# Gated projections of half a sequence as seven products of quarters instead of four plain ones per tile

## The chip, the cores and the metric

The kernel runs on one core of a Trainium2 chip. The metric is the device time of one execution in microseconds; the time before is the median of three runs. One further execution was profiled, and every row shown below comes from it. The engines are named as the profile names them: PE is TensorE, PEld its weight loads, DVE VectorE, ACT ScalarE, POOL GpSimd, SP the engine whose queue issues nearly all transfers.

## The reference

One decoder block on 2048 tokens of 1024 features, float32. What matters here is how two branches are joined:

```python
proj = h @ w_in[l]
q, k, v, z_a, u_b, v_b, z_b, g_logits = jnp.split(proj, SPLIT_IDX, axis=-1)
...
y_a = _swa_with_sinks(q, k, v, sinks[l]) * jax.nn.silu(z_a)      # 2048 x 512
y_b = ...  # spatial gating of u_b, v_b, times silu(z_b)          # 2048 x 512
gate_a, gate_b = jnp.split(jax.nn.sigmoid(g_logits), 2, axis=-1)
merged = gate_a * (y_a @ w_proj_a[l]) + gate_b * (y_b @ w_proj_b[l])
y = merged @ w_out[l]
x = x + gate * _rms(y, g_post[l])
```

## The kernel before

*Numbers.* Each float32 operand of a large product is split into a high part, rounded to the format that TensorE multiplies in, and a low part, the rest. A weight is split into a tile `W` (`w_of`: ScalarE casts the high part, L215; VectorE subtracts it for the low part, `sub`, L150), an activation into a tile `T` (`t_load`: casts at L373, subtractions at L150). A product of two 128x128 by 128x512 blocks is three matmuls: high by high, high by low, low by high (`mm3`, L167). The low part of `W` is first needed by the third.

*Stages.* The sequence is worked in two halves of 1024 tokens. (1) Two passes over `w_in`, one for each half, in 19 blocks of 256 output features. Each block is a product of 2x2 quarters by a scheme of seven products instead of eight (Strassen's, in Winograd's form): sums of quarters of the weight stand in `sS`, sums of quarters of the activation in `hT`; four PSUM banks X, Y, Z, W collect the products in the order of `BANK`, and ScalarE copies partial sums between banks (L418). The attention and the spatial gating of a half run beside its pass, hung on it with `later`. The last two blocks of a pass (`NLAST`) alternate product by product, with two banks each (`two_banks`), and the T tiles of what follows are loaded beside them. (2) The gated projections, first for the first half of the tokens, then for the second: the loop `for s in range(NS)` in `run_all`. (3) The output product with `w_out`, again by seven products, tile by tile of 128 rows of `merged` (`m_s`), with the norm and the final sum in `ev_out`.

*The projections.* For each of the eight feature tiles `j` there are four products of 12 matmuls: `y_a` and `y_b`, each for two groups of 512 tokens. One weight `W` serves two of them. When a product is done, `gated` (L1143) multiplies it on VectorE with one plus its gate tile; `g_load` has fetched the gate tiles into tags `m` and `e`. `merge` adds the gated `a` and `b` on VectorE and stores the sum to `m_s`. Four T tiles serve all eight `j`; the next four are loaded during the loop.

*Order.* Every engine works its own queue in the order in which the code emits instructions. One product is a *step*; `later(n, f)` emits `f` n steps on. At the start of step k the code takes the weight for it and prepares that of step k+3: ScalarE's cast is emitted then, VectorE's subtraction (`due`) one step later. There are four `W` buffers, eight for raw weights, ten for loads of T (`x`). Sums of weight quarters for a fresh (not stored) block are made by GpSimd in stage 3 (`psub`, L153).

Of the kernel before, what the change touches and what calls it, by code (L numbers as in the profile page):

```python
# [15 lines left out]
P = 128  # L16
D = 1024
# [38 lines left out]
def hybrid_block(ctx: ExitStack, tc: tile.TileContext, xt, x, wada, wgate, wI, wP, wO,  # L56
# [46 lines left out]
    sS = [[dram(f"sS{n}_{i}", [P, 512]) for i in range(4)] for n in range(NPAIR)]  # L103
    hT = [[dram(f"hT{p}_{kt}", [P, 512]) for kt in range(4)] for p in range(7)]
    oT = {p: [dram(f"oT{p}_{kt}", [P, 512]) for kt in range(4)] for p in (1, 2, 4, 6)}
# [207 lines left out]
    def presum(n):  # L313

        env, q = {}, wI_quads(n)
# [31 lines left out]
    for s in range(NS):  # L347
# [35 lines left out]
    class Block:  # L383
# [33 lines left out]
        def copy(self, to, of):  # L417
            act.copy(self.b[to], self.b[of])  # L418

# [706 lines left out]

    def o_src(p):
# [22 lines left out]
    def run_all():  # L1150
        nonlocal T

        for s in range(NS):
# [17 lines left out]
            if s == 0:  # L1171
# [5 lines left out]
                for i in range(NLAST):  # L1177
                    later(91 + 10 * i, lambda i=i: presum(NPAIR - NLAST + i))
            else:
                for kk in range(KT):  # L1180
# [3 lines left out]
                for kt in range(4):  # L1184
                    later(86 + 8 * kt, lambda kt=kt: o_step(kt))
# [65 lines left out]
        for s in range(NS):  # L1251
            Y4, nT = T, [None] * 7
            g_load(s, 0)
            for j in range(KT):
# [5 lines left out]
                for p in range(4):  # L1260
# [4 lines left out]
                    if s == 0:  # L1265
                        if j in (1, 2, 3) and p == 0:
                            t_load(nT, j - 1, 2, yab(1, j - 1))
                        elif j == KT - 1 and p == 0:
                            t_load(nT, 3, 1, yab(1, 3))
                    elif j in (2, 3, 4) and p == 0:  # L1270
# [24 lines left out]
    def ev_out(s, i):  # L1295
# [11 lines left out]
        def ev(key, src, psum):  # L1307
# [6 lines left out]
            if len(ys) == 2:  # L1314
                later(1, lambda: scale_of(r))

        def scale_of(r):
            xr, ss, ys = st[r]
            e0, v, ry = small(1, "e0"), small(1, "pw"), small(1, "ry")

            pool.tensor_scalar(out=e0, in0=ss[:, 0:1], scalar1=1.0 / D, scalar2=16.0 * EPS, op0=ALU.mult, op1=ALU.add)
            pool.tensor_scalar(out=v, in0=ss[:, 1:2], scalar1=1.0 / D, scalar2=e0, op0=ALU.mult, op1=ALU.add)
            pool.tensor_tensor(out=ry, in0=v, in1=nhalf[:, 0:1], op=ALU.pow)
            later(1, lambda: finish(r, ry))

        def finish(r, ry):
            xr, ss, ys = st[r]
            row = s * 8 + r * 4 + i
            for f in range(2):
# [90 lines left out]
```

## Time and profile before

| | |
|---|---|
| median of 3 runs | 1220.93 us (1220.47 to 1221.25) |
| the profiled execution | 1220.76 us, its span 1219.1 us, granted clock 0.997 |
| input pass, second half, to the first projection | until 885.1 us |
| projections, first half | 885.1 to 972.2 us |
| projections, second half | 972.2 to 1059.2 us |
| output product | 1059.2 to 1211.7 us |
| busy: TensorE, VectorE, ScalarE, GpSimd | 1199.3, 834.4, 607.5, 274.7 us |

A row of the timeline is the start, the duration, the engine, the line and operation, what it writes and reads, and how many equal ones it merges; in brackets stands the idle time before it and what ended it. Durations include a tail of some 0.08 us that overlaps with the next operation, so the spacing of starts tells what a queue costs. A matmul's duration is that of its way through the array: twelve that start 2.72 us before the next twelve are shown with 2.88.

### The profile page before, as it was taken

The numbers are of one execution on the slowest core, as the hardware profiler recorded it, in microseconds if no ns is written. First come the engines' busy times: TensorE is split into PE (matmuls) and PEld (weight loads), VectorE is DVE, ScalarE is ACT, GpSimd is POOL, SyncE is SP. The second block draws the span as 40 slices with busy tenths as digits, with TensorE's granted clock in tenths as the row PEclk, the third lists the DMA queues.
The fourth block names the chain that finished last, engine by engine and source line by source line (L and its number), as shares of the span: only waits on it lengthen the run. The fifth ranks groups of instructions, "written<-read, shape, count | busy, mean of one in ns | idle before, by whom it ended". The sixth has DMA issues, their size and how long they took to land.

```text
span 1219.1 us, 17154 instructions
## 1 busy us (share of the span) xinstructions
PE 1199.3 (98%) x5496; PEld 955.8 (78%) x5496; DVE 834.4 (68%) x1289; ACT 607.5 (50%) x1321; POOL 274.7 (23%) x246
## 2 busy tenths in 40 slices
PE   8999999999999999999999999999999999999997
PEld 3667887877777777888888787777788888888886
DVE  7996979667867666358757676555656556767775
ACT  4475454576765676434346665555622112444443
POOL 0002654323465200013200002210000000155443
PEclk9999999999999999999999999999999999999999
DMA  9545998867999996569795679888797677845452
GB/s 352 225 148 188 318 320 288 247 153 199 312 337 333 326 317 234 169 225 301 232 291 169 173 206 299 264 262 255 246 299 236 224 251 232 285 156 178 133 181 87
DMA packets 215506, 294.15 MB, mean 241 GB/s; under 512 B 19828, under 2 KB 96244, under 8 KB 215416
## 3 DMA queue, kind: packets, MB, share of 16 engines
q1 hardware_dynamic: 214944, 292.37, 74.7%
q8 instruction: 43, 0.70, 0.2%
q0 software_dynamic: 176, 0.53, 0.1%
q14 instruction: 47, 0.39, 0.1%
q10 hardware_dynamic: 296, 0.16, 0.1%
HBM read 189.50 MB, written 98.24 MB: 236 GB/s over the span
## 4 chain that ended last, share of the span: by engine, by line
PE 88%; DVE 5%; DMA 3%; ACT 2%; issue 1%; DVEq 0%; ACTq 0%; SPq 0%
PE bankY L167 28%; PE bankX L167 20%; PE bankW L167 12%; PE bankZ L167 12%; PE s L167 4%; PE b L167 4%; PE b L1009 2%; PE s L959 2%; DMA T<-in_wada 1%; PE s L960 1%; PE b L898 1%; PE b L994 1%; DVE W L150 1%; DMA raw<-in_wI 1%; DVE T L661 1%
## 5 line engine op out<-in xcount | busy, mean ns | idle before, releaser
L167 PE MATMUL bankY<-T,W 128*128 128x512 f32 x1608 | 390.5, 392 | 0.9 <-ACT bankZ L418 0.6
L167 PEld LDWEIGHTS bankY<-T,W 128*128 128x128 f32 x1608 | 299.3, 188 | 64.4 <-ACT bankZ L418 1.0
L150 DVE TENSOR_TENSOR W<-raw,W 128x512 fp32r<-128x512 f32 x320 | 255.1, 801 | 71.3 <-ACT W L215 71.1
L215 ACT CAST W<-raw 128x512 fp32r<-128x512 f32 x320 | 197.6, 618 | 169.5 <-PE b L167 53.2
L167 PE MATMUL bankX<-T,W 128*128 128x512 f32 x1140 | 279.7, 393 | 1.8 <-DVE T L661 1.7
L167 PEld LDWEIGHTS bankX<-T,W 128*128 128x128 f32 x1140 | 211.1, 188 | 48.1 <-DVE T L661 5.0
L167 PE MATMUL bankW<-T,W 128*128 128x512 f32 x708 | 175.8, 394 | 4.1 <-DVE T L661 2.5
L167 PE MATMUL bankZ<-T,W 128*128 128x512 f32 x708 | 171.0, 390 | 0.0
L167 PEld LDWEIGHTS bankW<-T,W 128*128 128x128 f32 x708 | 130.4, 188 | 36.5 <-DVE T L661 4.7
L167 PEld LDWEIGHTS bankZ<-T,W 128*128 128x128 f32 x708 | 132.2, 188 | 27.3
L153 POOL TENSOR_TENSOR S<-raw,raw 128x512 f32<-128x512 f32 x22 | 34.4, 1564 | 254.5 <-DMA raw<-m 200.0
L153 POOL TENSOR_TENSOR raw<-raw,raw 128x512 f32<-128x512 f32 x44 | 69.3, 1575 | 87.0 <-DVE W L150 36.6
L153 POOL TENSOR_TENSOR S<-x,x 128x512 f32<-128x512 f32 x18 | 24.5, 1366 | 218.9 <-DMA x<-in_wO 199.1
L156 DVE TENSOR_TENSOR e<-bankY,e 128x512 f32<-128x512 f32 x41 | 28.2, 689 | 63.7 <-PE bankY L167 63.6
L150 DVE TENSOR_TENSOR T<-x,T 128x512 fp32r<-128x512 f32 (+1 forms) x93 | 60.8, 695 | 9.7 <-ACT T L373 9.7
L167 PE MATMUL s<-T,W 128*128 128x512 f32 x276 | 66.4, 389 | 0.0
L167 PEld LDWEIGHTS s<-T,W 128*128 128x128 f32 x276 | 51.7, 188 | 10.7
L153 POOL TENSOR_TENSOR raw<-S,raw 128x512 f32<-128x512 f32 x22 | 32.3, 1469 | 116.8 <-DVE W L150 87.6
L373 ACT CAST T<-x 128x512 fp32r<-128x512 f32 x88 | 48.8, 618 | 4.2 <-PE s L167 4.2
L988 ACT ACTIVATE P<-P,rc 128x128 f32<-128x128 f32 x128 | 44.5, 396 | 11.4 <-DVE rc L984 11.1
L146 POOL TENSOR_SCALAR pw<-mv 128x1 f32<-128x1 f32 x16 | 6.6, 414 | 185.4 <-DVE mv L782 185.3
L979 ACT ACTIVATE P<-s,nb 128x129 f32<-128x129 f32 x128 | 46.0, 366 | 1.0 <-DVE nb L971 0.8
(236 smaller groups left out, 1380.9 us busy)
## 6 DMA issues: line engine op xcount, KB each, us to landing
raw<-in_wI SPq DMA_DIRECT2D x128, 256.0 KB, 4.3
raw<-sS SPq DMA_DIRECT2D x84, 256.0 KB, 4.4
g<-e SPq DMA_DIRECT2D x64, 256.0 KB, 3.9
sS<-raw SPq DMA_DIRECT2D x45, 256.0 KB, 4.4
T<-in_wada SPq DMA_DIRECT2D x16, 512.0 KB, 8.4
q<-q SPq DMA_DIRECT2D x64, 128.0 KB, 5.5
q<-k_s SPq DMA_DIRECT2D x64, 128.0 KB, 4.9
raw<-in_wP SPq DMA_DIRECT2D x32, 256.0 KB, 3.8
```

The source lines that it names most:

```text
L150: dve.tensor_tensor(out=o, in0=a, in1=b, op=ALU.subtract)
L153: pool.tensor_tensor(out=o, in0=a, in1=b, op=op)
L156: dve.tensor_tensor(out=o, in0=a, in1=b, op=ALU.add)
L167: pe.matmul(o, w[:, i, sl], t[:, j, kt, :], start=start and kt == kts[0] and n == 0, stop=stop and kt == last and n == 2, skip_group_check ...
L215: act.copy(w[:, 0, :], src)
L373: act.copy(T[p][:, 0, kt, :], rs[kt])
L661: dve.scalar_tensor_tensor(out=T[p][:, 1, kt, :], in0=t_src(p, kt), scalar=sh, in1=T[p][:, 0, kt, :].bitcast(F32), op0=ALU.add, op1=ALU.su ...
L898: pe.matmul(b[:, ch * P : (ch + 1) * P], st["v", h][:, ch, :], wT[:, c, :], start=True, stop=True)
L959: pe.matmul(o, q[:, g, :], k[:, 0, :], start=True, stop=False)
L979: act.activation(out=st["P", kv][:, g, :], in_=st["S", kv][:, g, 0 : P + 1], func=AF.Exp, scale=SM, bias=st["nb", kv][:, g : g + 1], accum ...
L988: act.activation(out=st["P", kv][:, g, 0:P], in_=st["P", kv][:, g, 0:P], func=AF.Copy, scale=st["rc", kv][:, g : g + 1])
L1009: pe.matmul(o[own, :], v[:, k, own], st["pv", kv][k], start=k == 1, stop=k == 0)
```

## The change

The projections of the first half (s = 0) are now made like the blocks of the passes. Features go in pairs of tiles (`Pair`, n = 0 to 3), tokens in two groups of 512, the inner dimension in two quarters of 256, so 2x2 quarters and seven products, each of six matmuls for `y_a` and six for `y_b`, side by side in banks of their own. Pairs 0 and 1 follow one another with four banks for each side, their weight sums made by GpSimd on the way; pairs 2 and 3 alternate with two banks for each side, their weight sums made earlier by `presum` (at steps 1 and 82 of the second pass) and stored. The sums of quarters of `y_a` and `y_b` (`pT`) are made by GpSimd in steps 9 to 20 of the second pass (`y_step`) and stored. The last two blocks of that pass now load seven T tiles instead of four. The sum of the two gated tiles moves from VectorE to GpSimd (`psub` in `out`), and gate tiles go into tags `m`, `S` and `q`. `o_step` is spread a little differently. In `ev_out` the two parts of the norm's sum are scaled by GpSimd as they come, and at the very end of the kernel the first row block is finished before the last multiplication. The projections of the second half stay as they were.

```diff
+    def p_quads(n):
+        return {f"A{f + 1}{k + 1}": wP[2 * n + f][:, :, 256 * k : 256 * (k + 1)].rearrange("a p c -> p a c")
+                for f in range(2) for k in range(2)}
...
-    for s in range(NS):
+    for n in range(2):
+        stream_fresh(p_quads(n))
+    for n in range(2, 4):
+        stream_stored(p_quads(n), NPAIR + n - 2)
+    by_product(2)
+    for s in range(1, NS):
...
+    class Pair:
...
+        def run(self, p, w, T):
+            early = self.two
+            if p >= 1 + early and p < 5 + early:
+                self.gates(("11", "22", "12", "21")[p - 1 - early])
+            if self.n == 0 and p == 0:
+                for z in "YZ":
+                    pe.matmul(self.b[1][z], w[:, 0, 0:P], T[p][:, 0, 0, :], start=True, stop=True, skip_group_check=True)
+            for ab in range(2):
+                mm3(self.b[ab][BANK[p]], w, T[p], (2 * ab, 2 * ab + 1), FRESH[p], True)
+                if ab == 0:
+                    do_hooks("mid")
...
+            elif p == 1:
+                self.wsb = [flat("e") for _ in both]
+                if self.two:
+                    dve.tensor_copy(self.wsb[0], self.b[0]["W"])
+                    act.copy(self.wsb[1], self.b[1]["W"])
+                    self.copy("Y", "X")
...
+            elif p == 3:
+                self.out("11", [self.b[ab]["X"] for ab in both])
+                if self.two:
+                    self.copy("Z", "Y")
+            elif p == 4:
+                c = [flat("e") for _ in both]
+                for ab in both:
+                    add(c[ab], self.b[ab]["Y"], self.wsb[ab])
+                self.out("22", c)
+            elif p == 5:
+                for ab in both:
+                    add(self.wsb[ab], self.b[ab]["Z"], self.wsb[ab])
+                self.out("12", self.wsb)
+            else:
+                self.out("21", [self.b[ab]["Y"] for ab in both])
...
+        def out(self, key, src):
+            ga, gb = (self.g.pop((key, ab)) for ab in range(2))
+            gated(ga, src[0])
+            gated(gb, src[1])
+            psub(ga, ga, gb, ALU.add)
+            store(1, m_s[half(key)][:, 2 * self.n + ft(key), :], ga)
...
+    def y_step(i):
+        hs = []
+        for k in (i % 2, i % 2 + 2):
+            for h in range(2):
+                hs.append(flat("x"))
+                sp.dma_start(hs[-1], (ya_s, yb_s)[i // 2][h][:, k, :])
+        keep_T(pT, i, hs, False, 3)
...
+                for i in range(4):
+                    later(6 + 3 * i, lambda i=i: y_step(i))
+                for i in range(2):
+                    later((1, 82)[i], lambda i=i: presum(NPAIR + i, p_quads(2 + i)))
...
-                elif p < 4:
-                    t_load(nT, p, 2, yab(0, p))
+                else:
+                    t_load(nT, p, 2, p_src(p))
...
+        for n in range(2):
+            c = banks()
+            blk = Pair(n, (BK, {"X": c[0], "Y": c[1], "Z": c[2], "W": c[3]}))
+            for p in range(7):
+                w = w_get()
+                step(lambda: blk.run(p, w, T))
+        c = banks()
+        blks = [Pair(2, (two_banks(BK["X"], BK["W"]), two_banks(BK["Y"], BK["Z"]))),
+                Pair(3, (two_banks(c[0], c[1]), two_banks(c[2], c[3])))]
+        nT = [None] * 7
+        for p in range(7):
+            if p < 4:
+                t_load(nT, p, 2, yab(1, p))
+            if p == 6:
+                g_load(1, 0)
+            for i in range(2):
+                w = w_get()
+                step(lambda: blks[i].run(p, w, T))
...
+            if r == 0 and s == NS - 1 and i == 3:
+                later(0, lambda: finish(r, ry), "mid")
+            else:
+                later(1, lambda: finish(r, ry))
```

What this does to the queues shows best where the pairs alternate. First TensorE. Before, in the projections of the first half; `s` and `b` are PSUM tiles beside the four fixed banks:

```order
L167 MATMUL bankX<-T_8355,W_8923 128x512 x12
L167 MATMUL bankY<-T_8439,W_8923 128x512 x12
L167 MATMUL bankZ<-T_8506,W_8975 128x512 x12
L167 MATMUL bankW<-T_8566,W_8975 128x512 x12
L167 MATMUL s_9139<-T_8355,W_9017 128x512 x12
```

Now, products 6 to 9 of the 14 of pairs 2 and 3 (counted from 0):

```order
L168 MATMUL bankX<-T_8712,W_9316 128x512 x6
L168 MATMUL bankY<-T_8712,W_9316 128x512 x6
L168 MATMUL s_9233<-T_8712,W_9351 128x512 x6
L168 MATMUL b_9234<-T_8712,W_9351 128x512 x6
L168 MATMUL bankW<-T_8778,W_9377 128x512 x6
L168 MATMUL bankZ<-T_8778,W_9377 128x512 x6
L168 MATMUL s_9233<-T_8778,W_9410 128x512 x6
L168 MATMUL b_9235<-T_8778,W_9410 128x512 x6
```

Twelve matmuls still share a weight, but the weight serves one step of twelve where it served two, and the T tile changes with every second step.

Then VectorE. Before, over the four products of a tile `j` beside which a T tile is split (`T<-x,T`):

```order
L1143 SCALAR_TENSOR_TENSOR m_8855<-m_8855,bankX 128x512
L150 TENSOR_TENSOR W_8881<-raw_8690,W_8881 128x512
L1143 SCALAR_TENSOR_TENSOR m_8859<-m_8859,bankY 128x512
L150 TENSOR_TENSOR T_8927<-x_8885,T_8927 128x512
L150 TENSOR_TENSOR T_8927<-x_8887,T_8927 128x512
L1143 SCALAR_TENSOR_TENSOR e_8856<-e_8856,bankZ 128x512
L150 TENSOR_TENSOR T_8927<-x_8889,T_8927 128x512
L150 TENSOR_TENSOR T_8927<-x_8891,T_8927 128x512
L150 TENSOR_TENSOR W_8923<-raw_8719,W_8923 128x512
L156 TENSOR_TENSOR m_8855<-m_8855,e_8856 128x512
L1143 SCALAR_TENSOR_TENSOR e_8860<-e_8860,bankW 128x512
L156 TENSOR_TENSOR m_8859<-m_8859,e_8860 128x512
```

Now, in products 8 and 9 of pairs 2 and 3, up to the split of the weight for product 12 (`W_9506`):

```order
L1236 SCALAR_TENSOR_TENSOR S_9417<-S_9417,e_9496 128x512
L1236 SCALAR_TENSOR_TENSOR q_9419<-q_9419,e_9497 128x512
L151 TENSOR_TENSOR W_9472<-raw_9318,W_9472 128x512
L151 TENSOR_TENSOR T_9476<-x_9401,T_9476 128x512
L151 TENSOR_TENSOR T_9476<-x_9403,T_9476 128x512
L157 TENSOR_TENSOR e_9529<-s_9233,e_9334 128x512
L157 TENSOR_TENSOR e_9530<-b_9235,e_9335 128x512
L1236 SCALAR_TENSOR_TENSOR S_9448<-S_9448,e_9529 128x512
L1236 SCALAR_TENSOR_TENSOR q_9450<-q_9450,e_9530 128x512
L151 TENSOR_TENSOR T_9476<-x_9405,T_9476 128x512
L151 TENSOR_TENSOR T_9476<-x_9407,T_9476 128x512
L151 TENSOR_TENSOR W_9506<-raw_9353,W_9506 128x512
```

The twelve rows of before belong to four products, the twelve of now to less than two. The sum of the gated tiles is gone from this queue and stands in GpSimd's, which had nothing between the sums for `w_out` and those for stage 3; these are the last two of pair 1 and the first four of pairs 2 and 3:

```order
L154 TENSOR_TENSOR m_9141<-m_9141,q_9143 128x512
L154 TENSOR_TENSOR S_9166<-S_9166,q_9168 128x512
L154 TENSOR_TENSOR m_9358<-m_9358,q_9360 128x512
L154 TENSOR_TENSOR m_9383<-m_9383,q_9385 128x512
L154 TENSOR_TENSOR S_9417<-S_9417,q_9419 128x512
L154 TENSOR_TENSOR S_9448<-S_9448,q_9450 128x512
```

Each of them follows a pair of gatings on VectorE, and the store of the sum follows it in SP's queue.

More of the change, by code (lines that the diff above doesn't have):

```diff
@@ L418, in copy, with __init__, gates @@
             act.copy(self.b[to], self.b[of])
+    class Pair:
+        def __init__(self, n, banks):
+            self.n, self.b, self.two = n, banks, banks[0]["W"] is banks[0]["Y"]
+            self.g = {}
+        def gates(self, key):
+            j, h = 2 * self.n + ft(key), half(key)
+            tags = ("m" if key[0] == "1" else "S", "q")
+            for ab in range(2):
+                t = self.g[key, ab] = flat(tags[ab])
+                sp.dma_start(t, g_s[8 * ab + j][h])
+        def run(self, p, w, T):
[5 more added lines that the diff above has]
+                    pe.matmul(self.b[1][z], w[:, 0, 0:P], T[p][:, 0, 0, :], start=True, stop=True, skip_group_check=True)
+            for ab in range(2):
+                mm3(self.b[ab][BANK[p]], w, T[p], (2 * ab, 2 * ab + 1), FRESH[p], True)
+                if ab == 0:
+                    do_hooks("mid")
+            both = range(2)
+            if p == 0:
+                if not self.two:
+                    self.copy("Y", "X")
[4 more added lines that the diff above has]
+                    act.copy(self.wsb[1], self.b[1]["W"])
+                    self.copy("Y", "X")
+                else:
+                    for ab in both:
+                        act.copy(self.wsb[ab], self.b[ab]["W"])
+            elif p == 2:
+                if not self.two:
+                    self.copy("Z", "Y")
+            elif p == 3:
+                self.out("11", [self.b[ab]["X"] for ab in both])
+                if self.two:
+                    self.copy("Z", "Y")
+            elif p == 4:
[4 more added lines that the diff above has]
+            elif p == 5:
+                for ab in both:
+                    add(self.wsb[ab], self.b[ab]["Z"], self.wsb[ab])
+                self.out("12", self.wsb)
+            else:
+                self.out("21", [self.b[ab]["Y"] for ab in both])
+        def copy(self, to, of):
+            for ab in range(2):
+                act.copy(self.b[ab][to], self.b[ab][of])
+        def out(self, key, src):
[4 more added lines that the diff above has]
+            store(1, m_s[half(key)][:, 2 * self.n + ft(key), :], ga)
@@ L1125, in yab, with p_src @@
         return [src[:, kt, :] for kt in range(4)]
+    def p_src(p):
+        if p in (1, 2, 4, 6):
+            return pT[p]
+        k, h = {0: (0, 0), 3: (1, 0), 5: (1, 1)}[p]
+        return [z[h][:, 2 * k + i, :] for z in (ya_s, yb_s) for i in range(2)]
+    def y_step(i):
[5 more added lines that the diff above has]
+        keep_T(pT, i, hs, False, 3)
     def o_src(p):
@@ L1184, in run_all @@
                 for kt in range(4):
-                    later(86 + 8 * kt, lambda kt=kt: o_step(kt))
+                    later(90 + 7 * kt, lambda kt=kt: o_step(kt))
             n0 = 0
@@ L1249, in run_all, with banks @@
             T = nT
-        for s in range(NS):
+        def banks():
+            S = pS.tile([P, 2, 512], F32, tag="s", name=nm("s"))
+            return S[:, 0, :], S[:, 1, :], bank(), bank()
+        for n in range(2):
[16 more added lines that the diff above has]
+                step(lambda: blks[i].run(p, w, T))
+        T = nT
+        for s in range(1, NS):
             Y4, nT = T, [None] * 7
-            g_load(s, 0)
             for j in range(KT):
@@ L1328, in finish @@
             row = s * 8 + r * 4 + i
-            for f in range(2):
+            for f in (r, 1 - r):
                 dve.scalar_tensor_tensor(out=xr[f], in0=ys[f], scalar=ry, in1=xr[f], op0=ALU.mult, op1=ALU.add)
```

33 lines of the change are left out of this document (16 added, 17 removed).

## The prediction

> **What bounds the kernel now.** I read the busy table and the chain first, then busy time by stage, then TensorE's rows in the stage that changes, and then VectorE's rows, because they show what could take TensorE's place.
>
> ```profile
> PE 1199.3 (98%) x5496; PEld 955.8 (78%) x5496; DVE 834.4 (68%) x1289; ACT 607.5 (50%) x1321; POOL 274.7 (23%) x246
> ...
> PE 88%; DVE 5%; DMA 3%; ACT 2%; issue 1%; DVEq 0%; ACTq 0%; SPq 0%
> ```
>
> TensorE is busy in 98% of the span and carries 88% of the chain. A matmul that goes away is time gained, unless TensorE then waits.
>
> ```profile
> 885.10:972.20 87.10, 87.10 (x386) 72.09 (x385) 50.25 (x78) 18.89 (x33) 0.00 (x0) 1.00 0.78 253
> ...
> 431.00:469.30 38.30, 38.30 (x175) 29.19 (x174) 30.87 (x54) 30.23 (x68) 0.00 (x0) 1.00 0.95 321
> ```
>
> The columns after the length are the busy time of TensorE, its weight loads, VectorE, ScalarE and GpSimd, then clock, share of the DMA engines and GB/s. 885 to 972 us is the projection stage of the first half: TensorE without a pause, VectorE at 58%, GpSimd idle. 431 to 469 us is the last pair of input blocks of the first half, fourteen products with seven T tiles loaded beside them: 321 GB/s at a share of 0.95, and still TensorE has no gap.
>
> ```profile
> 885.13 2.88 PE L167 MATMUL bankX<-T,W 128*128 128x512 f32 x12
> ...
> 969.46 2.88 PE L167 MATMUL b<-T,W 128*128 128x512 f32 x12
> 972.17 2.88 PE L167 MATMUL bankX<-T,W 128*128 128x512 f32 x12
> ```
>
> The first product of the stage starts at 885.13 and the first of the next stage at 972.17: 87.04 us for 32 groups of 12 matmuls, 2.72 us a group, 0.2267 us a matmul.
>
> **The change, part by part.**
>
> 1. *Matmuls.* Before, 8 feature tiles x 4 products x 12 = 384. After, 4 pairs x 7 products x 12 = 336, and 2 that only set up the banks Y and Z of the second side: 46 fewer. 46 x 0.2267 = 10.43 us less on TensorE, all of it on the chain.
>
> 2. *Sums of T, loads of T, sums of weights.* Sixteen GpSimd subtractions and eight weight sums move into the second input pass, and its last pair now loads seven T instead of four. The row of 431 us is that same load in the first half, T loads included, and it hid it. What is new there are four GpSimd sums for the first pair; each can take up to 1.10 us from VectorE (below), 4.4 us together, in 38.3 us of which VectorE was idle 7.4 (38.30 less 30.87). I take 0 and keep 1 us for the range.
>
> 3. *VectorE in the last two pairs.* This is the only stretch where I find it short. Pairs 2 and 3 alternate, 14 products. Call the start of the first one 0; product k ends at 2.72(k+1). VectorE has 14 splits of W, 16 of T, 16 gatings, 8 additions from PSUM and 2 copies: 56 operations. In a closed queue one follows another every 0.60 us, whatever it reads:
>
> ```profile
> 441.54 2.49 DVE L150 TENSOR_TENSOR T<-x,T 128x512 fp32r<-128x512 f32 x4
> 443.95 0.68 DVE L150 TENSOR_TENSOR W<-raw,W 128x512 fp32r<-128x512 f32 x1
> ...
> 460.98 1.28 DVE L150 TENSOR_TENSOR T<-x,T 128x512 fp32r<-128x512 f32 x2
> 462.18 0.68 DVE L156 TENSOR_TENSOR e<-bankY,e 128x512 f32<-128x512 f32 x1
> 462.78 1.28 DVE L150 TENSOR_TENSOR T<-x,T 128x512 fp32r<-128x512 f32 x2
> ```
>
> ```profile
> 1056.99 0.68 DVE L1143 SCALAR_TENSOR_TENSOR e<-e,s 128x512 f32<-128x512 f32 x1
> 1057.59 1.28 DVE L150 TENSOR_TENSOR T<-x,T 128x512 fp32r<-128x512 f32 x2
> ```
>
> Four splits of T take 443.95 - 441.54 = 2.41 us, the PSUM addition at 462.18 is followed at 462.78, the gating at 1056.99 at 1057.59. 56 x 0.60 = 33.6 of 38.1 us; but the splits of T lie in products 3 to 9 and all gatings come from product 6 on. The code hands VectorE the split of product m's W after the outputs of product m-3, and TensorE needs it at its third matmul, so the queue may run 5.4 + 0.45 us behind. From the end of product 6 (19.04, and 0.2 us until PSUM is read) to the split for product 12 stand 24 operations: 19.24 + 24 x 0.60 = 33.64, wanted at 12 x 2.72 + 0.45 = 33.09. TensorE waits 0.55. Each of the next two splits comes 5 operations (3.0 us) later where a product takes 2.72: 0.28 more each, 1.1 us in all. That is the low end.
>
> 4. *GpSimd's additions among them.* After each pair of gatings GpSimd now adds the two tiles (before, VectorE did, 0.60 us each). What that costs VectorE is in these rows:
>
> ```profile
> 593.71 5.95 POOL L153 TENSOR_TENSOR x<-x,m 128x512 f32<-128x512 f32 x4
> ...
> 595.03 1.77 DVE L156 TENSOR_TENSOR x<-x,x 128x512 f32<-128x512 f32 x1 [0.46 <-POOL x L153]
> 596.72 1.78 DVE L150 TENSOR_TENSOR W<-raw,W 128x512 fp32r<-128x512 f32 x1
> 598.42 1.77 DVE L806 TENSOR_TENSOR e<-e,m 128x512 f32<-128x512 f32 x1
> 600.12 0.67 DVE L870 SCALAR_TENSOR_TENSOR e<-e,bankX 128x512 f32<-128x512 f32 x1
> 600.72 0.68 DVE L150 TENSOR_TENSOR W<-raw,W 128x512 fp32r<-128x512 f32 x1
> ```
>
> While GpSimd worked through four operations on SBUF, VectorE's operations with both inputs in SBUF started 1.70 us apart instead of 0.60, one for each of GpSimd's: 1.10 us lost each time. One that reads PSUM loses nothing:
>
> ```profile
> 300.12 0.68 DVE L999 TENSOR_TENSOR m<-b,cst 128x512 f32<-128x512 f32 x1
> 300.17 1.29 POOL L153 TENSOR_TENSOR S<-x,x 128x512 f32<-128x512 f32 x1 [4.26 <-ACT x L1058]
> 300.83 0.69 DVE L150 TENSOR_TENSOR m<-b,m 128x512 f32<-128x512 f32 x1
> ```
>
> The two VectorE rows take 0.68 and 0.69 us under a GpSimd operation that runs from 300.17 to 301.46. Once in the trace it was GpSimd that waited:
>
> ```profile
> 1063.61 1.28 DVE L150 TENSOR_TENSOR T<-x,T 128x512 fp32r<-128x512 f32 x2
> 1063.82 4.63 POOL L153 TENSOR_TENSOR raw<-raw,raw 128x512 f32<-128x512 f32 x1 [14.96 <-DVE W L150]
> ...
> 1065.41 1.28 DVE L150 TENSOR_TENSOR T<-x,T 128x512 fp32r<-128x512 f32 x2
> 1066.62 0.68 DVE L150 TENSOR_TENSOR W<-raw,W 128x512 fp32r<-128x512 f32 x1
> 1068.41 1.29 POOL L153 TENSOR_TENSOR S<-raw,raw 128x512 f32<-128x512 f32 x1
> ```
>
> Here VectorE's queue was closed, its operations stayed at 0.68 or 1.28 for two, and GpSimd's took 4.63 us, until the queue had a gap. So the price of an addition lies between 0 and 1.10 us. Four of the eight come before the split for product 12 and meet splits of T and W with both inputs in SBUF; the four after it meet additions from PSUM. I take 1.10, because the slowed rows recur and the other stands alone: 4 x 1.10 = 4.4 us, and the wait grows from 1.1 to 5.5 us. [...]
>
> 5. *PSUM copies.* Each pair needs 2 copies from X to Y, 2 of W out and 2 from Y to Z on ScalarE.
>
> ```profile
> 1054.56 4.32 ACT L373 CAST T<-x 128x512 fp32r<-128x512 f32 x8
> ...
> 1062.13 0.57 ACT L418 COPY bankY<-bankX 128x512 f32<-128x512 f32 x1 [1.06 <-PE bankX L167]
> ```
>
> A copy takes 0.57 us and eight casts of T 4.32, so 0.54 each. In the interleaved pairs the W and Y copies after a product (3 x 0.57) have the partner's product, 2.72 us, to hide in, with at most two casts of T between them: 1.71 + 0.54 + 0.2 = 2.45. The Z copies wait for the gatings of product 6; with VectorE not yet late there they are ready at about 21.1, the next product wants them at 21.76. For product 9 they come 0.1 to 0.2 us late, which the 5.5 us already hold, since VectorE's queue runs on meanwhile. Pairs 0 and 1 do not alternate, but have four banks for each side; the second side of pair 1 starts when the last gating of pair 0 has read its bank, about when TensorE arrives (20.4 us from the start of pair 0 by both counts). I take 0 and keep 0.8 for the range.
>
> 6. *The end.*
>
> ```profile
> 1208.81 2.88 PE L167 MATMUL bankY<-T,W 128*128 128x512 f32 x12
> ...
> 1211.40 0.55 POOL L1323 TENSOR_TENSOR ry<-pw,nhalf 128x1 f32<-128x1 f32 x1
> ...
> 1212.51 0.69 DVE L1313 TENSOR_TENSOR e<-bankY,rg 128x512 f32<-128x512 f32 x1 [1.33 <-ACT m L1311]
> 1212.57 0.19 POOL L1321 TENSOR_SCALAR e<-yss 128x1 f32<-128x1 f32 x1 [0.62 <-ACT m L1311]
> 1212.86 0.26 POOL L1322 TENSOR_SCALAR pw<-yss,e 128x1 f32<-128x1 f32 x1
> 1213.12 2.73 DVE L1330 SCALAR_TENSOR_TENSOR x<-e,ry,x 128x512 f32<-128x512 f32 x4
> 1213.21 1.06 POOL L1323 TENSOR_TENSOR ry<-pw,nhalf 128x1 f32<-128x1 f32 x1
> ```
>
> The last matmul ends at 1211.69. VectorE then does one multiplication (1212.51) and four final operations (1213.12 to 1215.85), though the factor of the first two was ready at 1211.95. Now these two stand ahead of the multiplication, and GpSimd's tail is an operation shorter (0.29 us from 1212.57 to 1212.86): the last factor is there at 1213.98 instead of 1214.27, and 2 x 0.68 later, at 1215.35, all is done. That gains 0.5 us; the bounds are 0 and 0.8.
>
> Sum, on the profiled execution's 1220.76 us (span 1219.1): -10.43 + 5.5 - 0.5 = -5.4. The median of the runs is 0.17 above that execution: 1220.93 - 5.4 = 1215.5 us.
>
> **The rivals.**
>
> *GpSimd yields.* Its additions fall into VectorE's gaps, as at 1063.82; the wait is 1.1 us. 1220.93 - 10.43 + 1.1 - 0.5 = 1211.1. Against it stand the three rows from 595 on.
>
> *The DMA queue fills.* In products 4 to 11 of the alternating pairs some 37 transfers of 262 KB start (16 gates, 8 T, 8 weights, 5 stores), 9.7 MB. At the rate of the 431 us row (321 GB/s at 0.95, so 338 full) that takes 28.7 us where 21.8 pass: up to 6.9 us late.
>
> ```profile
> m<-g SPq DMA_DIRECT2D x32, 256.0 KB, 3.6
> ...
> m<-m SPq DMA_DIRECT2D x32, 256.0 KB, 2.8
> ...
> x<-ya SPq DMA_DIRECT2D x16, 256.0 KB, 5.2
> ```
>
> T loads start 5.4 us ahead and took 5.2, so they have no reserve; but ScalarE reaches their casts later than that (the second T some 8 us after its load), and nothing needs these T before the next stage. Half of the lateness, 3.4 us, on top of the sum: 1218.9.
>
> *Slower than before: gates behind stores.* SyncE's queue is in order. A store of a sum waits for GpSimd, which waits for VectorE, and the next gate loads stand behind it; VectorE in turn stops at a gating whose gate has not landed, with the splits of W behind that. A loop of landing (3.6), store and wait could put VectorE further back at every product. TensorE must lose 10.9 us before the change is slower than nothing, so 5.4 beyond part 4; with the full 6.9 us late at the gates it ends at 1222.4. For it: each gate tile of a pair has a store ahead of it. Against it: the first gates are asked for in product 4 and used after product 6, 8.2 us ahead of a landing of 3.6, and the later ones are wanted by a VectorE that is itself late.
>
> **How the numbers follow.** My forecast, additions at full price: 0.48. GpSimd yields: 0.27. The DMA queue: 0.14. The loop: 0.07. What I do not see: 0.04. A difference under 0.2% (2.4 us) can't be told from none. The forecast and the yielding case lie beyond that, with half of the DMA case: 0.82 faster; most of the rest of the DMA case and part of the unseen, 0.10, the same; the loop and the rest, 0.08, slower. The range runs from 1210.5, just under the yielding case with the end at its best, to 1219.0, over the DMA case; it leaves out the loop, the upper part of the DMA case and a little below, 0.18 together.
>
> **What would show it.** Right: the products of the four pairs 2.72 us apart but for gaps in TensorE from product 12 of the alternating pairs on, released by the split of W on VectorE, 4 to 6 us in all; splits there 1.7 us apart beside GpSimd's additions; no gap in the second input pass; the final four operations done about 3.7 us after the last matmul instead of 4.2. No gaps there and GpSimd additions of several us would be the first rival; gaps released by ScalarE's casts of T or by loads the second; gatings that wait for gate loads the third. The forecast is wrong, too, if TensorE waits in the first two pairs, where I see none.

## The result and the profile after

The changed kernel takes 1229.36 us (median of 4 runs, 1228.62 to 1230.78) beside 1220.72 us for the kernel before on the same chip: ratio 1.0072, 95% interval 1.0054 to 1.0089. It is slower by 0.7%; faster by 0.4% was forecast. The profiled execution took 1228.62 us, its span 1226.9 us.

The busy row of the page, and the view of TensorE's waits (who waits, for whom, us in total, times, longest). The four shown have no counterpart in the profile of before:

```profile
PE 1199.8 (98%) x5450; PEld 953.9 (78%) x5450; DVE 863.2 (70%) x1315; ACT 631.8 (51%) x1367; POOL 348.0 (28%) x294
```

```profile
PE b L856 <- DMA q<-vb: 4.2, 1, 4.2
PE s L168 <- DVE e L157: 3.1, 1, 3.1
PE b L924 <- ACT S L928: 3.1, 1, 3.1
...
PE s L168 <- DVE q L1236: 1.4, 1, 1.4
```

TensorE issues 46 matmuls fewer (5450 for 5496) and is busy no less: 1199.8 us for 1199.3. So the matmuls that are left take longer somewhere. These four waits add up to 11.8 us, and lie in two places, the second input pass and the pairs. First TensorE's timeline of the pass, now and before:

```profile
526.08 3.02 PE L168 MATMUL bankX<-T,W 128*128 128x512 f32 x12
533.28 1.09 PE L856 MATMUL b<-cst,q 128*128 128x128 f32 x4 [4.19 <-DMA q<-vb]
534.02 5.05 PE L168 MATMUL bankW<-T,W 128*128 128x512 f32 x12
542.19 1.12 PE L924 MATMUL b<-cst,e 128*128 128x128 f32 x4 [3.11 <-ACT S L928]
542.96 4.09 PE L168 MATMUL bankY<-T,W 128*128 128x512 f32 x12
546.88 2.89 PE L168 MATMUL bankX<-T,W 128*128 128x512 f32 x12
```

```profile
526.79 3.02 PE L167 MATMUL bankX<-T,W 128*128 128x512 f32 x12
...
536.04 2.88 PE L167 MATMUL bankX<-T,W 128*128 128x512 f32 x12
```

The changed kernel comes to this place 0.71 us ahead and leaves it 10.84 us behind: 11.55 us lost in 20. Of these 7.3 are the two waits (for the first load of `v`, and for the copy of a `v` block out of PSUM). The rest is in the durations: twelve matmuls behind the waits take 5.05 and 4.09 us instead of 3.0. The windows say why; the columns are as in the prediction, clock, DMA share and GB/s at the end. Now and before:

```profile
530.00:540.00 10.00, 5.79 (x16) 4.42 (x16) 3.38 (x4) 0.62 (x1) 8.75 (x8) 0.66 0.95 318
...
535.20:537.20 2.00, 2.00 (x7) 1.52 (x6) 0.89 (x2) 0.00 (x0) 2.00 (x3) 0.50 1.02 320
```

```profile
530.00:540.00 10.00, 10.00 (x51) 8.29 (x50) 7.39 (x11) 5.26 (x10) 3.98 (x4) 1.00 0.48 155
```

The clock granted behind the wait is 0.50. The DMA engines move twice the bytes of before, and GpSimd is busy for 8.75 of 10 us.

In the pairs, at the boundary from pair 0 to pair 1 and in the alternating pairs:

```profile
918.38 1.66 PE L168 MATMUL s<-T,W 128*128 128x512 f32 x6 [1.39 <-DVE q L1236]
...
964.96 1.52 PE L168 MATMUL bankY<-T,W 128*128 128x512 f32 x6
969.62 2.90 PE L168 MATMUL s<-T,W 128*128 128x512 f32 x6 [3.14 <-DVE e L157]
972.32 2.76 PE L168 MATMUL b<-T,W 128*128 128x512 f32 x6
...
980.74 2.88 PE L168 MATMUL bankX<-T,W 128*128 128x512 f32 x12
```

The stage runs from 895.98 (its first, setting-up matmul) to the first product of the next stage at 980.74: 84.76 us for 87.04 before. It saves 2.28 of the 10.43 that the matmuls are worth. Some 1.7 us go at 916.8, where side b of pair 1 waits for the last gating of pair 0, and 6.4 us from product 11 on (964.96 is side b of product 10): a pause of 3.3, then two groups of six matmuls that are followed by the next after 2.70 and 2.56 us instead of 1.36 (2.90 and 2.76 in the rows, tail included). From 964.96 to the next stage at 980.74 pass 15.78 us, where seven groups of 1.36 make 9.52.

From there the two kernels run alike to the last matmul (1208.81 before, 1217.38 now, 8.57 apart), and the new end gains 0.77: the spans are 7.8 apart. Sum: 11.55 - 0.71 - 2.28 - 0.77 = 7.8 us.

### The profile page after: what moved, and what is told of

It is laid out like the page before. It is cut to its first block, busy times and chain, and to the rows that moved or that the text cites. A ratio compares the mean times of both kernels' runs of the same rounds, so it can differ in the third digit from the quotient of the medians.

```text
span 1226.9 us, 17364 instructions
## 1 busy us (share of the span) xinstructions
PE 1199.8 (98%) x5450; PEld 953.9 (78%) x5450; DVE 863.2 (70%) x1315; ACT 631.8 (51%) x1367; POOL 348.0 (28%) x294
## 4 chain that ended last, share of the span: by engine, by line
PE 84%; DVE 6%; DMA 5%; ACT 2%; issue 1%; POOL 1%; SPq 0%; DVEq 0%; ACTq 0%; POOLq 0%
PE bankY L168 27%; PE bankX L168 19%; PE bankW L168 11%; PE bankZ L168 11%; PE s L168 4%; PE b L168 3%; PE b L1088 2%; PE s L1038 2%; DMA T<-in_wada 1%; PE s L1039 1%; DVE W L151 1%; PE b L977 1%; PE b L1073 1%; DMA raw<-sS 1%; DMA raw<-in_wI 1%
## 5 line engine op out<-in xcount | busy, mean ns | idle before, releaser
L151 DVE TENSOR_TENSOR W<-raw,W 128x512 fp32r<-128x512 f32 x330 | 263.7, 804 | 81.4 <-ACT W L216 81.1
L216 ACT CAST W<-raw 128x512 fp32r<-128x512 f32 x330 | 203.6, 618 | 144.5 <-PE b L168 42.8
L154 POOL TENSOR_TENSOR S<-x,x 128x512 f32<-128x512 f32 x28 | 37.5, 1345 | 304.2 <-DMA q<-q 119.4
L154 POOL TENSOR_TENSOR raw<-raw,raw 128x512 f32<-128x512 f32 x48 | 76.2, 1588 | 98.8 <-DVE W L151 47.0
L151 DVE TENSOR_TENSOR T<-x,T 128x512 fp32r<-128x512 f32 (+1 forms) x105 | 75.5, 762 | 8.5 <-ACT T L384 8.3
L154 POOL TENSOR_TENSOR S<-raw,raw 128x512 f32<-128x512 f32 x24 | 37.6, 1566 | 142.3 <-DMA raw<-in_wI 56.4
L168 PE MATMUL s<-T,W 128*128 128x512 f32 x282 | 71.0, 396 | 4.5 <-DVE e L157 3.1
L384 ACT CAST T<-x 128x512 fp32r<-128x512 f32 x100 | 55.9, 619 | 2.7 <-PE s L168 2.1
L429 ACT COPY bankZ<-bankY 128x512 f32<-128x512 f32 x42 | 24.0, 571 | 46.0 <-PE bankY L168 45.9
L408 ACT COPY e<-bankW 128x512 f32<-128x512 f32 x41 | 23.9, 584 | 44.7 <-PE bankW L168 42.1
```

Source lines behind the costliest of these rows:

```text
L151: dve.tensor_tensor(out=o, in0=a, in1=b, op=ALU.subtract)
L154: pool.tensor_tensor(out=o, in0=a, in1=b, op=op)
L168: pe.matmul(o, w[:, i, sl], t[:, j, kt, :], start=start and kt == kts[0] and n == 0, stop=stop and kt == last and n == 2, skip_group_check ...
L216: act.copy(w[:, 0, :], src)
L384: act.copy(T[p][:, 0, kt, :], rs[kt])
L408: act.copy(self.wsb, b["W"])
```

## The experiments

All are the changed kernel (1229.4 us) with the edit shown, but for the one on pauses, which edits the kernel before and is not in the table, since it ran once. In the rows, SPq is SP's queue at the issue of a transfer.

| kernel | us | to the kernel before, 95% interval |
|---|---|---|
| changed kernel | 1229.36 | 1.0072 (1.0054 to 1.0089) |
| tables on ScalarE's queue | 1225.76 | 1.0041 (1.0026 to 1.0056) |
| sums of y 40 steps later | 1232.41 | 1.0096 (1.0081 to 1.0111) |
| banks of pair 3 | 1228.95 | 1.0072 (1.0057 to 1.0087) |
| additions on VectorE | 1229.99 | 1.0080 (1.0063 to 1.0097) |
| sums of y in place | 1224.05 | 1.0033 (1.0020 to 1.0045) |
| sums of y spread | 1217.77 | 0.9977 (0.9967 to 0.9986) |
| late T, X in b | 1224.50 | 1.0033 (1.0020 to 1.0047) |
| tables on ScalarE and in place | 1219.92 | 0.9992 (0.9982 to 1.0002) |
| both cures | 1212.99 | 0.9935 (0.9921 to 0.9950) |
| both, T at 4 and 6 | 1214.00 | 0.9946 (0.9932 to 0.9961) |
| both, T ahead of the gate | 1212.32 | 0.9927 (0.9914 to 0.9941) |

### The second pass: tables on ScalarE's queue

```diff
-  later((18, 12)[s], lambda s=s: load_rope(s))
+  later((18, 4)[s], lambda s=s: load_rope(s))
   # in load_rope, second half: act.dma_start, two a step from step 5 on, instead of sp.dma_start
```

> The 16 small transfers for the rotation tables of the second half (m<-cs) are issued by ScalarE, two a step from step 5 of the pass on, instead of 16 at once by SP in step 12; all else as in the changed kernel (1229.4 us). Theory Q, SP's queue: the first load of v (q<-vb) stands in SP's in-order queue behind these 16 transfers (10.75 us of issue) and behind the loads and stores of the sums of y_a and y_b. Then both waits of TensorE in the second input pass (4.19 us for q<-vb, 3.11 us at the v transposes) and the slow matmuls behind them go: 1229.4 - 11.6 = 1217.8 us, and q<-vb lands before 522 us instead of 530. Rival D, the DMA engines: 360 GB/s were moved between 520 and 530 us, and the same bytes still have to be moved; then the time stays within 2 us of 1229.4 and q<-vb still lands after 526 us. If only the first of the two waits hangs on SP, about 6 us go and 1223 remains.

Measured: 3.6 us less, not 11.6. SP's queue in the changed kernel, then the load of `v` before the change and in this run, then what TensorE and ScalarE wait for in this run:

```profile
500.72 10.75 SPq L798 DMA_DIRECT2D m<-cs  x16
...
520.75 2.20 SPq L1217 DMA_DIRECT2D x<-yb  x4
...
526.67 0.90 SPq L850 DMA_DIRECT2D q<-vb  x1
```

```profile
518.72 0.57 SPq L771 DMA_DIRECT2D q<-vb  x1
```

```profile
525.07 0.53 SPq L855 DMA_DIRECT2D q<-vb  x1
```

```profile
532.10 0.63 PE L861 MATMUL b<-cst,q 128*128 128x128 f32 x4 [0.93 <-DMA q<-vb]
...
539.31 0.66 PE L929 MATMUL b<-cst,e 128*128 128x128 f32 x4 [3.84 <-ACT S L933]
```

```profile
538.67 0.59 ACT L933 COPY S<-b 128x512 f32<-128x512 f32 x1 [8.15 <-DMA pT<-S]
```

With the 10.75 us of table transfers out of SP's queue the load of `v` is issued only 1.6 us earlier (525.07 for 526.67). The expectation had the mechanism wrong: the tables are not what holds SP. The first wait shrank from 4.19 to 0.93 partly because TensorE itself came 2.1 us later; 0.94 of that is a wait for a bank copy that ScalarE, busy issuing, made late. The second wait stayed, and its releaser is named now: the copy of `v` needs an `S` tile, and the `S` tiles are held until the stores `pT<-S` of the sums of y have landed.

### The second pass: the sums of y in another place

```diff
-  later(6 + 3 * i, lambda i=i: y_step(i))
+  later(46 + 4 * i, lambda i=i: y_step(i))          # 40 steps later
+  later((6, 11, 57, 64)[i], lambda i=i: y_step(i))  # spread
```

> The loads, sums and stores of the quarters of y_a and y_b are hung 40 steps later in the second input pass (steps 46, 50, 54, 58 instead of 6, 9, 12, 15); all else as in the changed kernel (1229.4 us). Both theories of the second pass, SP's queue and the DMA engines, expect both waits between 526 and 547 us to go: 1229.4 - 11.6 = 1217.8 us. What tells is the second wait: by the reading that it comes from the S tiles that the sums hold until their stores land, it goes here even if the first one stayed (1225). Rival: the sums only carry their waits along to the new place, and the time stays near 1229.

> The four sets of sums of y_a and y_b are hung at steps 6, 11, 57 and 64 of the second pass instead of 6, 9, 12, 15, so that two are done before the loads of v begin, five steps apart (154 GB/s more each, on some 140), and two lie near 640 to 680 us, where the kernel before moved 190 to 200 GB/s. All else as in the changed kernel (1229.4 us). Theory B, bytes: both waits between 526 and 547 us go, and the new places have room: 1229.4 - 11.6 = 1217.8, within 1.5 us. Theory Q, in-order queue and shared S tiles (as when the sums stood at steps 46 to 58, where SP stopped at a load into an S tile and the loads of k behind it came 8.7 us late): the first two waits go, but at steps 57 to 70 TensorE waits for loads of k or v again, 3 to 10 us: 1221 to 1228.

Measured: 40 steps later, the two waits are gone and the time is 3 us *worse*. SP and TensorE there:

```profile
646.97 1.94 SPq L1174 DMA_DIRECT2D S<-in_wgate  x2
...
652.88 1.26 SPq L1022 DMA_DIRECT2D q<-k_s  x2
```

```profile
659.64 0.55 PE L1038 MATMUL s<-q,q 128*128 128x256 f32 x1 [8.74 <-DMA q<-k_s]
```

The loads of `k` stand behind loads into `S` tiles and behind four of y (issued from 644.48 on, 2.41 us), and TensorE waits 8.74 us; another 2.3 wait for `vn`. The expectation had this only as a rival: the sums carry their waits along. Spread out, with two sets where the kernel before had room, the whole 11.6 us come back: 1217.77 for 1217.8 expected. The load of `v` is issued at 521.42 there, though the tables are still ahead of it, and no wait is left in this stretch:

```profile
521.42 0.57 SPq L850 DMA_DIRECT2D q<-vb  x1
```

### The second pass: tiles, queue or bytes

```diff
-  st[key] = flat("S")                       # keep_T
-  psub(st[key], a, ...); store(2, dst[p][kt], st[key])
+  psub(o, a, b); store(2, dst[p][kt], o)    # o one of the four loaded x tiles
```

> The sums of the quarters of y_a and y_b are written over the loaded x tiles instead of into S tiles; places, loads and stores stay (changed kernel 1229.4 us). Theory S, tiles: the copy of v on ScalarE (L928 of the changed kernel, S<-b) stops TensorE for 3.11 us because the four S tiles are held by sums whose stores have not landed; with no S tile in the sums this wait and the slow matmuls behind it go, and the one for q<-vb stays: 1229.4 - 5 = 1224.5 us. Theory B, bytes: three steps of 2.72 us carry 2.1 MB for one set of sums, 257 GB/s on top of the 134 to 157 that the kernel before moved there, more than the 360 GB/s that were ever reached; then everything in this stretch is late whatever tiles it uses, and 1227 to 1231 remains.

> In the second pass, the rotation tables by ScalarE's queue and the sums of y_a and y_b in place, so that neither SP's queue nor the S tiles hold the first loads and copies of v; the bytes and the steps in which the sums are made stay (6, 9, 12, 15). Theory Q and S (queue order for the first wait, S tiles for the second): both waits go but for 0.9 us that were left with the tables on ScalarE, 1225.8 - 5 = 1220.5, or 1229.4 - 3.6 - 5.4 = 1220.4. Theory B, bytes (400 GB/s wanted where 360 were the most): the same 2.1 MB in 8.2 us stay too much, loads land 7 us and more after their issue, and TensorE still waits 4 us or more in this stretch, 1223 to 1226.

In place alone: 1224.05, where 1224.5 was expected. The copy of `v` in the changed kernel, then here, and TensorE here:

```profile
541.55 0.58 ACT L928 COPY S<-b 128x512 f32<-128x512 f32 x1 [9.80 <-POOL x L154]
```

```profile
532.60 0.58 ACT L928 COPY S<-b 128x512 f32<-128x512 f32 x1
```

```profile
534.24 1.09 PE L856 MATMUL b<-cst,q 128*128 128x128 f32 x4 [3.58 <-DMA q<-vb]
```

TensorE no longer waits at L924: the second wait hangs on the `S` tiles. (In the changed kernel the releaser named is a GpSimd operation on other tiles, the last thing in that queue to end; it isn't the cause, since here the copy, at 532.60, runs ahead of that operation, which starts at 537.49.) The first wait stays at 3.58.

In place and with the tables on ScalarE, 1219.92, as the theory of queue and tiles had it (1220.4), though SP's queue carries the same sums, in the same steps. A window shows that the bytes alone are not what stops TensorE:

```profile
530.00:540.00 10.00, 9.34 (x45) 7.48 (x45) 5.90 (x8) 5.06 (x10) 4.79 (x5) 1.00 1.02 354
```

The DMA engines are full (1.02 here, 1.01 to 1.03 from 510 to 550 us), and TensorE waits 0.66 for the load of `v`, and nowhere else in these 40 us. Nor are 360 GB/s the most, as the theory of bytes took it: with the sums in place alone, 378 GB/s were moved from 530 to 540 us. Most of the first wait comes from the late issue. Before, the load of `v` was issued at 518.72, 8 us earlier; from its issue at 526.67 to the matmul that waits for it pass 6.6 us, where such loads took 3.5 to 5.2 us to land before (510 to 560 us). How much of the late issue is the plain order of SP's queue and how much the waits of that queue for transfers in full DMA engines was not separated: the spread takes both away.

### The pairs: which wait, and VectorE's lag

```diff
-  Pair(3, (two_banks(c[0], c[1]), two_banks(c[2], c[3])))]
+  Pair(3, (two_banks(c[0], c[2]), two_banks(c[1], c[3])))]   # banks of pair 3
-  psub(ga, ga, gb, ALU.add)
+  add(ga, ga, gb)                                            # additions on VectorE
```

> In pair 3 the four half tiles of PSUM are dealt out otherwise: X and Z of both sides lie in the two halves of the shared tile s, Y and W in the two tiles b, instead of side a in s and side b in the b tiles. All else as in the changed kernel (1229.4 us). Theory T, shared tile alone: TensorE stops at product 11 only because its write of Z (one half of s) waits for VectorE's read of Y (the other half); then the wait of 3.14 us and the slow products after it go, 1229.4 - 6.4 = 1223.0. Theory L, VectorE's lag: VectorE is some 5 us late there in any case, and the wait only moves from the tile to the split of the weight of product 12, as the prediction had it: that split comes near 974.1 where product 12 would want it at 969.3, so a wait of 4 to 5 us for W, released by VectorE line 151, and 1228 to 1231 us.

> The sum of the two gated tiles in the pairs goes back from GpSimd to VectorE; all else as in the changed kernel (1229.4 us). If a GpSimd addition costs VectorE 1.10 us as predicted while its own addition costs 0.60, VectorE's splits of T take 1.28 for two again, the reading of Y that TensorE waits for comes about 1.5 us earlier (three additions before it, 0.5 us each), the wait at product 11 shrinks from 3.14 to some 1.6 us and the slow products behind it shrink with it: 1225.5 to 1227.5 us. [...]

The banks of pair 3 dealt otherwise: 1228.95, no change, as the theory of VectorE's lag had it. TensorE now passes product 11 and stops inside product 12, at the third matmul:

```profile
972.97 2.08 PE L168 MATMUL bankW<-T,W 128*128 128x512 f32 x4 [3.97 <-DVE W L151]
```

So the wait at product 11 of the changed kernel (3.14 us) is VectorE's lag, met one product early: its Z and its Y are halves of one PSUM tile, and TensorE's write of one waits for VectorE's read of the other.

The lag also decides where the stage ends, and not the slow matmuls behind the pause. In the kernel with the sums 40 steps later the same pause left the clock at 1.00 (973.6 to 976.6 us), and six matmuls behind it took 1.63 us instead of 2.90:

```profile
973.67 1.63 PE L168 MATMUL s<-T,W 128*128 128x512 f32 x6 [3.14 <-DVE e L157]
...
981.98 1.60 PE L168 MATMUL s<-T,W 128*128 128x512 f32 x6 [1.14 <-DVE e L157]
...
984.78 2.88 PE L168 MATMUL bankX<-T,W 128*128 128x512 f32 x12
```

There TensorE waited 1.16 for the split of `W` in product 12 and 1.14 for the shared tile again at product 13. From side b of product 10 (969.01) to the next stage 15.77 us passed, as in the changed kernel (15.78). The four other kernels that keep these pairs as they are, with the clock at one half for shorter or longer, lie at 15.75 to 15.78; only with the banks of pair 3 dealt otherwise, behind the longer pause, it is 16.52.

VectorE at that place in the changed kernel, GpSimd's addition, and the same splits with the additions on VectorE:

```profile
966.08 1.64 POOL L154 TENSOR_TENSOR S<-S,q 128x512 f32<-128x512 f32 x1 [3.63 <-DVE q L1236]
```

```profile
966.52 2.35 DVE L151 TENSOR_TENSOR T<-x,T 128x512 fp32r<-128x512 f32 x2
968.80 0.68 DVE L157 TENSOR_TENSOR e<-s,e 128x512 f32<-128x512 f32 x1
...
973.49 0.68 DVE L151 TENSOR_TENSOR W<-raw,W 128x512 fp32r<-128x512 f32 x1
```

```profile
968.40 1.28 DVE L151 TENSOR_TENSOR T<-x,T 128x512 fp32r<-128x512 f32 x2
```

Two splits take 2.35 us beside GpSimd and 1.28 without: the price of 1.1 is confirmed, by taking its cause away. Yet the kernel is no faster (1229.99, where 1225.5 to 1227.5 was expected). It waits 1.79 at product 11, then 0.82 for a split of `W`, then 1.86 at product 13, with the clock at full, and needs 14.80 us for the stretch of 15.78. But 1.2 us are lost ahead of it, 0.84 of them where pair 2 waits for the last gating of pair 1, and the stage takes 85.01 us for 84.76. All eight additions of the two pairs now cost VectorE 0.6 each; on GpSimd only the half that meets splits costs anything (1.1 each).

### The pairs: T later, and the boundary

```diff
-  if p < 4: t_load(nT, p, 2, yab(1, p))
+  loads 0, 1 at p = 0, 1 (n = 2); load 2 at p = 5 (n = 2); load 3 at p = 6 (n = 1)
-  blk = Pair(n, (BK, {"X": c[0], "Y": c[1], "Z": c[2], "W": c[3]}))
+  blk = Pair(n, (BK, {"X": c[2], "Y": c[0], "Z": c[1], "W": c[3]}))
```

> Two edits at different places of the trace. In pairs 2 and 3 the loads of T tiles 2 and 3 of the next stage, with their casts and splits, are hung at products p = 5 and 6 instead of 2 and 3, so that VectorE has four splits fewer before the reading of Y. In pairs 0 and 1 side b keeps X and W in the two b tiles and Y and Z in the shared s tile. All else as in the changed kernel (1229.4 us). Theory L, VectorE's lag: its queue is some 5 to 6 us shorter at product 11 (four splits of T at 1.2 each), the wait of 3.14 us and the slow products after it go, -6.4. Rival: the same operations are only late a little further on, and TensorE waits for T at the first products of the next stage instead, 0 to -3. The swap takes the wait of 1.39 us at the first product of pair 1 away, -1.6, if it comes from the shared tile, and nothing if the gatings themselves are late. By the first of each: 1229.4 - 6.4 - 1.6 = 1221.4 us.

4.9 us less, where 8.0 were expected. Products 10 to 13 run without a gap; 1.5 us of it are given back in two waits at the third product of the next stage, as the rival said; the first of them:

```profile
981.69 0.97 PE L168 MATMUL bankZ<-T,W 128*128 128x512 f32 x3 [0.72 <-DVE T L151]
```

The wait at the boundary went (-1.39), but the last Y of pair 0 then waited for the read of Z in the shared tile (1.03): the deal with X and Z together, used below, has neither.

### How long a pause, how slow after

```diff
+  if s == 1 and p == 0 and j in (1, 3, 5):
+      z = flat("q")
+      for _ in range({1: 1, 3: 4, 5: 8}[j]): act.copy(z, last[0])
+      pe.matmul(bk[0][:, 0:P], z[:, 0:P], z[:, 0:P], start=True, stop=True, ...)
```

> The kernel before (1220.9 us), with three pauses of TensorE put into the projections of the second half, some 21 us apart, where its products follow without a gap at full clock: ahead of the first product of tiles 1, 3 and 5, a small matmul waits for 1, 4 and 8 copies on ScalarE (0.5 us each) of the bank that TensorE has just finished. Theory C, the clock: after a pause of some us TensorE's granted clock falls for the products behind it, as the rows behind the pauses of 3.1 and 4.2 us in the changed kernel suggest (twelve matmuls in 5.05 instead of 3.02 us); then the pause of about 1 us costs itself alone, those of about 2.5 and 4.5 us cost themselves and 1.5 to 3.5 us more, with a granted clock of 0.5 to 0.8 in the rows behind. Rival: the slow products in the changed kernel came from the crowded DMA engines or from late operands, and here the products after a pause start 2.72 us apart at once, with a clock of 1.00.

Each pair of rows is the small matmul that ends the pause and the twelve behind it; then the clock of the two microseconds behind the first two pauses:

```profile
983.12 0.49 PE L1281 MATMUL s<-q 128*128 128x128 f32 x2 [1.40 <-ACT q L1280]
983.36 3.01 PE L167 MATMUL s<-T,W 128*128 128x512 f32 x12
...
1008.95 0.49 PE L1281 MATMUL s<-q 128*128 128x128 f32 x2 [3.54 <-ACT q L1280]
1009.19 4.59 PE L167 MATMUL s<-T,W 128*128 128x512 f32 x12
...
1039.58 0.79 PE L1281 MATMUL s<-q 128*128 128x128 f32 x2 [6.76 <-ACT q L1280]
1040.03 4.68 PE L167 MATMUL s<-T,W 128*128 128x512 f32 x12
```

```profile
983.40:985.40 2.00, 2.00 (x11) 1.66 (x11) 0.00 (x0) 0.00 (x0) 0.00 (x0) 1.00 0.71 235
1009.20:1011.20 2.00, 2.00 (x8) 1.58 (x8) 0.00 (x0) 0.00 (x0) 0.00 (x0) 0.58 0.71 195
```

The one run took 1237.22 us. A pause of 1.40 us costs itself. One of 3.54 or 6.76 (2.5 and 4.5 were meant) costs some 1.6 us on top, the same for both (4.59 and 4.68 for 3.01): the clock stands near one half for the next 4 us (0.58 and 0.56 in two windows of 2 us behind the second pause, 0.50 and 0.58 behind the third). No crowded DMA engine is needed for it: their share is 0.71 behind the first pause and the second.

### Both cures

```diff
+  later((6, 11, 57, 64)[i], lambda i=i: y_step(i))
+  T loads 2 and 3 at p = 5 (n = 2) and 6 (n = 1)
+  blk = Pair(n, (BK, {"X": c[0], "Z": c[1], "Y": c[2], "W": c[3]}))
```

> The two cures together: sums of y_a and y_b at steps 6, 11, 57 and 64, T loads 2 and 3 of the next stage at products 5 and 6 of pairs 2 and 3; and in pairs 0 and 1 side b keeps X and Z in the shared s tile, Y and W in the b tiles, so that the shared tile's last reader is the sum from Z, one product ahead of the last gating. If the losses are independent they add up: 1217.8 (spread alone) - 4.4 (late T alone took 4.9 with 0.5 of it at the boundary) - 1.5 (the boundary) = 1212, within 1.5 us. Rival: with 11 us less ahead of them the gate and T loads of the pairs collide otherwise, and less than 3 of the 6 us come: 1214.5 to 1217.

1212.99 us: faster than the kernel before by 0.65% and than the changed one by 16.4 us. The cures add up. The stage of the pairs takes 77.10 us (885.32 to 962.42), where 87.04 - 10.43 = 76.6 was to be had. What is left is 1.5 us at the third product of the next stage. VectorE reaches the splits of that T behind a gating whose gate tile is late:

```profile
964.40 0.69 DVE L1236 SCALAR_TENSOR_TENSOR S<-S,bankW 128x512 f32<-128x512 f32 x1 [3.71 <-DMA S<-g]
...
966.40 2.38 DVE L151 TENSOR_TENSOR T<-x,T 128x512 fp32r<-128x512 f32 x2
```

Two variants of that order:

> As the kernel with both cures, but T load 2 at product 4 instead of 5, because with it at product 5 VectorE reached its splits only after a gating that waited 3.9 us for its gate tile, and TensorE then waited 1.5 us at the third product of the next stage. If that is so, those waits go and nothing new comes in products 10 to 13: 1 to 1.5 us less than with product 5, near 1210.7. Rival: the two splits (1.2 each beside GpSimd) come back ahead of the sums from Y and the splits of W, and TensorE waits there: 0.5 to 3 us more than with product 5.

> As the kernel with both cures (spread sums, T loads 2 and 3 at products 5 and 6; 1213.0 us), but the cast and the splits of T tile 2 come one step earlier (n = 1), so that its first two splits stand ahead of the gating that waits 3.7 us for its gate tile instead of behind it. If the 1.5 us that TensorE waits at the third product of the next stage come from that order alone, they go: 1211.5. Rival: ScalarE's cast now comes 2.72 us after the load is asked for, where loads take some 5 us to land, holds the casts of W and the copies between banks behind it, and TensorE waits at products 12 or 13 instead: 1212.5 to 1215.

With T load 2 at product 4 the rival came true, 1 us more: the two splits are back ahead of the sums from Y, and TensorE waits 3.21 at product 13 and 1.19 for a split of `W`. With the splits ahead of the late gating, that T is in time, but the split of `W` that now stands behind the same gating is late:

```profile
969.31 2.56 PE L168 MATMUL bankZ<-T,W 128*128 128x512 f32 x10 [1.17 <-DVE W L151]
```

1212.32, 0.7 us less, with intervals that overlap, and above the 1211.5 that was expected: it is the late gate tile that holds VectorE, whatever stands behind it. Why that tile is late was not tried, nor were both cures with the additions back on VectorE.

## Why the prediction was wrong

It was 13.9 us too low (1215.5 for 1229.36). In the profiled executions the terms are: 11.55 in the second pass, 2.65 in the pairs (8.15 lost for 5.5), less 0.27 at the end and less 0.71 by which this execution was ahead by the second pass (why is open), 13.2 together; the rest is that it lies 0.7 under the median of its runs, and the one before 0.2.

- *Part 1, the matmuls.* Right: 10.43 us; with the waits cured 9.9 of them come.
- *Part 2, the sums and loads in the pass, "I take 0".* This step failed, and alone turned the sign. It priced what GpSimd's sums cost VectorE and the T loads of the last pair, and passed over the 16 loads and 16 stores of the sums of y: 2.1 MB for each set, three steps (8.2 us) apart, 257 GB/s on top of 134 to 267 in the same stretch of before. They hold the `S` tiles until their stores land, stand in SP's queue ahead of the loads of `v`, and TensorE stops twice. The cover that it named, the row of 431 us, stands for the last pair of the pass, and there TensorE did run without a gap; the sums of y lie in another stretch. Undone by the spread: 11.6 us.
- *Parts 3 and 4, VectorE's lag.* Mechanism right, and the size nearly: 1.1 us for each addition beside splits of T; nothing beside operations that read PSUM (0.68 and 0.67 us at 977.09 and 977.70, under an addition that ran from 976.65 to 978.32). The split of `W` for product 12 was forecast 38.0 us after the start of the alternating pairs, 974.2, and ran from 973.49 to 974.17. Moving the additions back to VectorE left the time where it was (1229.99 for 1229.36, with intervals that overlap). Missed was that the two halves of a PSUM tile are waited for as one. That put the first wait at product 11 and made another at product 13, where the sum had 0.28: 6.3 us in all for 5.5. The slow matmuls behind the pause add nothing to it, since with the clock at full the same stretch took as long.
- *Part 5, the boundary, 0 with a bound of 0.8.* It cost 1.7, by the same shared tile. The bound was too small; copies on ScalarE did hide.
- *Part 6, the end.* 0.77 gained, forecast 0.5 with bounds 0 to 0.8.
- *The rivals.* GpSimd did not yield; the DMA queue and the loop at the gates were not what bound the changed kernel, though a late gate shows once the others are cured. The rival that came true, SP's queue and the tiles behind it, had been looked for in the pairs alone.

## What to carry to other kernels

Work that is hung beside a stage must be priced there, with all it issues: the bytes against the GB/s of that very stretch, its place in the in-order queue against the next load that has a deadline, and the tiles that it holds until its stores land. VectorE's queue, busy all of the 15 us from 965 on, was cured by moving work that had no deadline yet (the splits of T); where the additions stood, on VectorE (1229.99) or on GpSimd (1229.36), made no difference to the time. In these runs some pauses of TensorE slowed the matmuls behind them. That cost 1.6 us on top of the pause where TensorE alone set the pace, in the run with the three pauses, and nothing where another engine was later still, in the pairs (15.78 us with the slow matmuls, 15.77 without).

## What the runs showed of the hardware

The granted clock fell to 0.50 after some pauses, during them or up to 1 us behind them, and came back after some 3 to 6 us of matmuls: in the changed kernel it fell 2.5, 2.8 and 2.1 us into the pauses of 4.19, 3.11 and 3.14 us and came back 5.2, 3.1 and 5.7 us behind their ends (read from windows of 0.5 us). From the first pass on, pauses of up to 1.86 us left it at 1.00. Those of 3.54 us and more (up to 8.74) halved it, one of 3.84 only 1 us behind its end. In between it went both ways. Pauses of 1.97 (late T), 2.17 (banks of pair 3) and 2.69 us (additions on VectorE), all at the copy of `v` and begun less than 2 us after the clock had come back from a longer pause, halved it. So did those of 3.11 and 3.14 us in the changed kernel. One of 2.30 us and the one of 3.14 us with the sums 40 steps later did not, nor did one of 3.21 us (both cures with T at 4 and 6, product 13):

```profile
961.85 1.61 PE L168 MATMUL s<-T,W 128*128 128x512 f32 x6 [3.21 <-DVE e L157]
```

So between 2 and 3.2 us the length alone does not decide.
